# Sums of squares of the first norm on TensorE, and one rounding copy for both streams

## The chip, the cores and the metric

The kernel runs on one core of one Trainium2 chip. A core has a matrix engine (TensorE, PE in the profile, with its weight loads shown apart as PEld), VectorE (DVE), ScalarE (ACT), GpSimd (POOL), and SyncE (SP), whose queue issues the DMAs here. Each engine works through its own list in order and waits on semaphores of the others. The metric is device time of one execution in microseconds (us); lower is better.

## The reference

Two layers of a transformer-like trunk over 256 latent tokens and 256 context tokens of 1024 features, in fp32. Each layer is feed-forward, mixer, feed-forward. Every sublayer begins with a norm and a modulation:

```python
def rms_norm(x, g):
    y = x32 * lax.rsqrt(jnp.mean(x32 * x32, axis=-1, keepdims=True) + RMS_EPS)
    return (y * g.astype(jnp.float32)).astype(x.dtype)

def ffn_sublayer(h, m, g, w13, w2, base):
    hn = modulate(rms_norm(h, g), m[:, :, base], m[:, :, base + 1])   # h * (1 + scale) + shift
    return h + 0.5 * m[:, :, base + 2] * swiglu(hn, w13, w2)
```

The shifts, scales and gates m come from the conditioning vectors: `silu(cond) @ w + b`, one set for the latent tokens, one for the context tokens. The change is about the very first norm only, that of the first feed-forward of layer 0, which treats both streams together.

## The kernel before

Features lie on the 128 partitions, tokens along the row: `xl_all` holds the latent tokens as 8 d-tiles of 128x256, `xc_all` the context tokens. A matmul operand is split into a rounded part (`xh`, `whi`) and the rest (`xl`, `wlo`), and `mm3` makes three matmuls of them (L242 to L244).

The first feed-forward (`ffn_first`) begins while the inputs are still landing. Its list on ACT, DVE, PE and SP is written by hand in the order of the code (`tc.manual_schedule`); POOL's is not. It does this:

- `spread_c` puts the silu of the conditioning vectors on every partition as rows (PE transposes of L166, copies to `cvec`).
- `mod_cols(l, s, i, q, raw)` makes shift i and scale i of stream q (0 latent, 1 context). It consists of two calls of `mod_half`, each a DVE reduction over a 128x1024 weight tile (L197, out `jk`) and a short read of its accumulator; the second is followed by a small operation that makes the gain column `g` or `gc` (L204). Tile `mr` is the weight tile, from SP's DMAs.
- `squares(q, ...)` sums x*x over the features. ACT squares two halves of four d-tiles (L369, into `sq`). Then eng, POOL for the latent stream and DVE for the context stream, adds the d-tiles up (L373 to L376) until one 128x256 tile is left. `Rstd` sums its partitions with a matmul against a column `ones`, one per block of 128 tokens (L254), takes the root on ACT (L264), the reciprocal on DVE (L265), spreads it to all partitions with two transposes (L272) and copies it to `rs2` (`rs` in the profile, L279).
- `unit(k, q)` multiplies d-tile k of stream q by that (DVE, L386, into `xn`). `modulated(k)` applies gain and shift on ACT, first twice into the rounded `xh` (L392), then twice in place into the fp32 `xn` (L395). `low_part(k)` makes `xl` on DVE (L398). `split_hi` and `split_lo` split a quarter of the weight chunk of k (L406, L411).
- The loop over the 8 k-tiles (operand k for 8 column blocks at once): six blocks are fp32 matmuls of `xn` with the raw weights (L477, two instructions per matmul), two are `mm3` (outputs `p_3a`, `p_3b`). Ahead of the matmuls of k, each round writes unit, split and modulation of k + 1 and the modulation columns of k + 2.

`squares` is a generator: each `next` issues its next piece, so that other work can be put between. PSUM tiles come from two pools, three of two banks (`pair`) and two of one (`single`). After the loop come the rest of the first feed-forward (`pa`, `py`), the even mixer, two feed-forwards, the odd mixer, a last feed-forward and the final norm, which the change leaves as they are; their weight blocks are rounded on ACT by L98 and on DVE by L99.

Of the kernel before, what the change touches and what calls it, by code (L numbers as in the profile page):

```python
# [17 lines left out]
P = 128  # L18
# [33 lines left out]
def out_order(n, late):  # L52
    """Blocks (d, k) of an output projection: for the first n d-tiles the k-tile that is there last comes last."""
    early = [(d, k) for d in range(n) for k in range(KD) if k != late] + [(d, late) for d in range(n)]
    return early + [(d, k) for d in range(n, KD) for k in range(KD)]
# [6 lines left out]
class Stream:  # L62
    """Weight blocks in order of use: loaded two chunks at a time, then split into two float32r parts."""

# [41 lines left out]
    def block(self):  # L106
        """The next block of a run of blocks that starts with a chunk."""
        if self.at_chunk():
            self.run = self.get()
        j = self.blk % CH  # L110
        self.blk += 1
        return self.run[0][:, j, :], self.run[1][:, j, :]
# [3 lines left out]
def hybrid_trunk_kernel(ctx: ExitStack, tc: tile.TileContext, xc, cols_d, modw, wst, poolw_d,  # L116
# [15 lines left out]
    def single(name):  # L132
        return ps1.tile([P, 512], F32, tag="single", name=name)

    W = Stream(nc, wp_raw, wp_s, wst, 6, 3)

# [1 line left out]
    cols = cp.tile([P, NCOL], F32, name="cols")  # L138
# [16 lines left out]

    # silu of the conditioning vectors, as a row on every partition
    cvec = cp.tile([P, 2, D], F32, name="cvec")
# [16 lines left out]

# [1 line left out]
    mcol = {}  # L176
# [14 lines left out]
    def mod_half(l, s, i, q, h, raw):  # L191
        """Pairs 0..7 are (shift_i, scale_i); pairs 8..11 are gates (2(i-8), 2(i-8)+1)."""
        j = (i, 8 + i)[h] if i < 8 else 16 + 2 * (i - 8) + h
        m = mcol[l, s, q]
        junk = mp.tile([P, D], BF16, tag="junk", name=f"jk{l}{s}{i}{q}{h}", bufs=1)
        b = C_MODB + 72 * l + 24 * s + j
        nc.vector.tensor_tensor_reduce(  # L197
            out=junk, in0=raw[:, h, :], in1=cvec[:, q, :], scale=1.0,
            scalar=cols[:, b : b + 1], op0=ALU.mult, op1=ALU.add,
            accum_out=m[:, j : j + 1],  # L200
        )
        if h == 1 and i < 8:
            g0 = C_G + 24 * l + 8 * s + i
            nc.vector.scalar_tensor_tensor(  # L204
                gcol[l, s, q][:, i : i + 1], m[:, 8 + i : 9 + i], 1.0,
                cols[:, g0 : g0 + 1], ALU.add, ALU.mult,
            )
        elif i >= 8 and s != 1:
            nc.vector.tensor_scalar_mul(m[:, j : j + 1], m[:, j : j + 1], 0.5)
# [17 lines left out]
    def mod_credit(columns):  # L227
        """Issue modulation work for about so many columns per partition."""
        have[0] += columns
        while todo and have[0] >= 2 * len(todo[0][3]):  # L230
            have[0] -= 2 * len(todo[0][3])
            mod_next()

    def need_mods(l, s, lo, hi):
        """All columns of these pairs are issued by now."""
        while any(t[:2] == (l, s) and lo <= t[2] < hi for t in todo):
            mod_next()

# [1 line left out]
    def mm3(out, w, x, first, last):  # L240
# [5 lines left out]
    class Rstd:  # L246
        """Sums of squares over the d-tiles -> reciprocal root mean square of each token, on all partitions."""

# [10 lines left out]
        def root(self):  # L259
            """Tokens are on partitions here."""  # L260
            with tc.high_priority(offset=URGENT):
# [6 lines left out]
        def rows(self):  # L268
            """On all partitions, in PSUM."""
            n = self.n  # L270
# [12 lines left out]
    class Act:  # L283
        """Operand parts of one sublayer: columns 0..255 and a shift column twice, for one or two streams."""

# [12 lines left out]
        def feed(self, d, q=0):  # L298
            """Once x[d] is there."""
            with tc.high_priority(offset=URGENT):  # L300
# [41 lines left out]

# [1 line left out]
    def ffn_first():  # L344
        with tc.tile_pool(name="g0", bufs=1) as gp:
# [17 lines left out]

            def squares(q, xs_all, eng):
                """Yields after each piece of work, so that the caller can place it."""
                ts = []
                for h in range(2):
                    t = wp_s.tile([P, 4, T], F32, tag=("whi", "wlo")[h], name=f"sq4{q}{h}")
                    nc.scalar.activation(t, xs_all[:, 4 * h : 4 * h + 4, :], AF.Square)  # L369
                    ts.append(t)  # L370
                yield
                for t in ts:
                    eng.tensor_tensor(t[:, 0:2], t[:, 0:2], t[:, 2:4], ALU.add)  # L373
                eng.tensor_tensor(ts[0][:, 0:2], ts[0][:, 0:2], ts[1][:, 0:2], ALU.add)
                acc = ts[0][:, 2, :]
                eng.tensor_tensor(acc, ts[0][:, 0], ts[0][:, 1], ALU.add)  # L376
                yield
                Rstd([acc], 256, f"00{q}", None, q).root().spread()
                yield

            def unit(k, q):
                """x times its reciprocal root mean square"""
                if q == 0:
# [4 lines left out]
            def modulated(k):  # L388
                for q in range(2):
                    g, sh = gcol[0, 0, q][:, k : k + 1], mcol[0, 0, q][:, k : k + 1]  # L390
                    h = xh[:, k, q * 256 : q * 256 + 256]
                    nc.scalar.activation(h, xn[k][:, q, :], AF.Identity, bias=sh, scale=g)  # L392
                for q in range(2):
                    g, sh = gcol[0, 0, q][:, k : k + 1], mcol[0, 0, q][:, k : k + 1]
                    nc.scalar.activation(xn[k][:, q, :], xn[k][:, q, :], AF.Identity, bias=sh, scale=g)  # L395

            def low_part(k):
# [26 lines left out]
            with tc.manual_schedule(engines=MANUAL):  # L424
# [9 lines left out]
                spread_c()  # L434
                lat, con = squares(0, xl_all, nc.gpsimd), squares(1, xc_all, nc.vector)
                next(lat)
                mod_cols(0, 0, 0, 0, raws[0])
                next(lat)
                next(con)
                mod_cols(0, 0, 0, 1, raws[0])  # L440
                next(con)
                next(lat)
                mod_half(0, 0, 1, 0, 0, raws[1])
                unit(0, 0)
                next(con)
                mod_half(0, 0, 1, 0, 1, raws[1])
                unit(0, 1)
                prs = [pair(f"p0_{j}") for j in range(3)]
                pts = [t[:, j, :] for t in prs for j in range(2)] + [single("p0_3a"), single("p0_3b")]
                split_hi(0)  # L450
                modulated(0)
                split_lo(0)
                mod_half(0, 0, 1, 1, 0, raws[1])
                low_part(0)
                mod_half(0, 0, 1, 1, 1, raws[1])
                for k in range(KD):
# [5 lines left out]
                    if not last:  # L462
                        for q in range(2):
                            unit(k + 1, q)
                        split_hi(k + 1)
                        modulated(k + 1)
                        if k + 2 < KD:
# [63 lines left out]

# [1 line left out]
    def even_mixer(act):  # L533
        with tc.tile_pool(name="mix", bufs=2) as ap_:
# [51 lines left out]

            # windowed means less the token, then the per-group map
            def pool_means():
# [38 lines left out]
            def put(name, i, t, n):  # L627
                """t [P, n streams, 258] with its shift column -> float32r parts, tokens along the row."""
                h = ap_.tile([P, n * T], F32R, tag=f"{name}h", name=f"{name}h{i}")
# [44 lines left out]
            def scores(i, b):  # L674
                """Scores of two heads, and the steps of their softmax."""
                (qh, ql), (kh_, kl_) = qs[i], ks_[i]
# [68 lines left out]

            # first pair of heads: the norm's factor is still under way
            wq, wk = W.get(), W.get()
# [87 lines left out]
    class OutProj:  # L835
        """Output projection of a mixer; the operand's last k-tile may come late."""

# [34 lines left out]

# [1 line left out]
    def ffn(act, l, s, gp, nxt_of, rate1, rate2):  # L874
# [43 lines left out]

# [1 line left out]
    def odd_mixer(act, gp, rate):  # L920
# [70 lines left out]
def _blocks(w, cols):  # L991
    """w (1024, n) -> [len(cols), 128, 8 * 128]: chunk per group of 128 output features, k-tiles along the row."""
    import numpy as np
# [121 lines left out]
```

## Time and profile before

| | |
|---|---|
| median of three executions | 1209.8 us (1209.5, 1209.8, 1213.49) |
| the profiled execution, its span | 1211.3 us |
| mean granted TensorE clock | 0.986 |
| first norm: POOL's four adds (L373 to L376) | 9.73 to 16.26 us |
| first matmul of the loop over k (L477) | 23.20 us |
| DVE's reductions L197, whole program | 184, 236.4 us |

The page of the profile gives busy times by engine, the chain of work that ended last and groups of like instructions. A row of the timeline reads: start in us from the span's beginning, duration in us, engine, line, operation, output<-inputs, shape, count of merged instructions, and in brackets the idle time before it with what ended it. A row of waits reads: who waited <- for whom: us in total, times, longest. The profile merges neighbours of one line, so the step between them is worked out from a row's length and count. "Granted clock" is the share of full speed that TensorE's clock gate passed; where the trace has no record yet (before 7.6 us) the column shows 1.00.

### The profile page before, as it was taken

How to read it: one execution, taken by the hardware profiler on the slowest of the kernel's cores; microseconds unless marked ns; L12 is line 12 of the kernel's file. 1: busy time of each engine (PE TensorE's matmuls, PEld its weight loads, DVE VectorE, ACT ScalarE, POOL GpSimd, SP SyncE). 2: the span in 40 equal slices, each digit the busy share in tenths (PEclk: the TensorE clock that was granted, in tenths of full speed). 3: DMA queues.
4: the chain of work that ended last, by engine and by line, in shares of the span. 5: the costliest groups of instructions: out<-in, count | busy, mean ns of one | idle time of the engine just before them, and what ended most of it. 6: DMA issues, size and time to landing. Idle time of an engine off the chain costs nothing.

```text
span 1211.3 us, 19831 instructions
## 1 busy us (share of the span) xinstructions
PE 1180.3 (97%) x8134; PEld 1084.0 (89%) x8134; DVE 918.6 (76%) x1463; ACT 535.7 (44%) x804; POOL 21.2 (2%) x23
## 2 busy tenths in 40 slices
PE   4999999999999999999999999999999999999997
PEld 2568888888888988999999999999999999999997
DVE  8967686676788697877887897887887887676653
ACT  4352321223234444655544545454545456545542
POOL 2000000000000040000000000000000000000000
PEclk7999999999999999999999999999999999999999
DMA  7755454356666653235667886766786555554551
GB/s 275 247 212 173 173 176 174 139 215 272 244 259 229 223 133 88 70 125 213 226 236 256 307 334 219 256 228 243 281 322 232 174 182 191 185 174 180 195 182 35
DMA packets 45801, 250.72 MB, mean 207 GB/s; under 512 B 12944, under 2 KB 13328, under 8 KB 17552
## 3 DMA queue, kind: packets, MB, share of 16 engines
q1 hardware_dynamic: 45712, 249.48, 57.6%
q8 instruction: 63, 1.03, 0.3%
q14 instruction: 26, 0.21, 0.0%
HBM read 248.41 MB, written 1.05 MB: 206 GB/s over the span
## 4 chain that ended last, share of the span: by engine, by line
PE 94%; DVE 2%; DMA 1%; issue 1%; ACT 0%; SPq 0%; DVEq 0%; ACTq 0%
PE pf L243 11%; PE pf L242 10%; PE pf L244 10%; PE pa L243 6%; PE pa L242 6%; PE pa L244 6%; PE pz L244 5%; PE pz L243 5%; PE pz L242 5%; PE p L477 4%; PE py L243 3%; PE py L244 3%; PE py L242 3%; PE pwo L242 1%; PE pwo L243 1%; PE pc L243 1%
## 5 line engine op out<-in xcount | busy, mean ns | idle before, releaser
L98 ACT CAST whi<-raw 128x1024 fp32r<-128x1024 f32 x312 | 327.1, 1049 | 460.6 <-PE pa L243 121.0
L99 DVE TENSOR_TENSOR wlo<-raw,whi 128x1024 fp32r<-128x1024 f32 x312 | 380.2, 1223 | 177.1 <-ACT whi L98 176.5
L242 PE MATMUL pf<-ah,whi 128*128 128x258 f32 x1056 | 298.4, 283 | 0.0
L243 PE MATMUL pf<-al,whi 128*128 128x258 f32 x1056 | 298.4, 283 | 0.0
L244 PE MATMUL pf<-ah,wlo 128*128 128x258 f32 x1056 | 297.6, 282 | 0.0
L197 DVE CUSTOM_DVE_ANT_0 jk<-mr,cvec,cols 128x1024 bf16<-128x1024 f32 x184 | 236.4, 1285 | 1.7
L244 PEld LDWEIGHTS pf<-ah,wlo 128*128 128x128 f32 x1056 | 200.2, 190 | 0.0
L243 PEld LDWEIGHTS pf<-al,whi 128*128 128x128 f32 x1056 | 200.1, 190 | 0.0
L242 PEld LDWEIGHTS pf<-ah,whi 128*128 128x128 f32 x1056 | 199.7, 189 | 0.0
L243 PE MATMUL pz<-gl,whi 128*128 128x256 f32 x528 | 148.3, 281 | 0.0
L244 PE MATMUL pz<-gh,wlo 128*128 128x256 f32 x528 | 148.3, 281 | 0.0
L242 PE MATMUL pz<-gh,whi 128*128 128x256 f32 x528 | 148.3, 281 | 0.0
L243 PE MATMUL pa<-xl,whi 128*128 128x512 f32 x288 | 114.0, 396 | 0.0
L242 PE MATMUL pa<-xh,whi 128*128 128x512 f32 x288 | 113.7, 395 | 0.0
L244 PE MATMUL pa<-xh,wlo 128*128 128x512 f32 x288 | 113.6, 394 | 0.0
L242 PEld LDWEIGHTS pz<-gh,whi 128*128 128x128 f32 x528 | 99.5, 188 | 0.0
L244 PEld LDWEIGHTS pz<-gh,wlo 128*128 128x128 f32 x528 | 99.5, 188 | 0.0
L243 PEld LDWEIGHTS pz<-gl,whi 128*128 128x128 f32 x528 | 99.5, 188 | 0.0
L243 PE MATMUL py<-gl,whi 128*128 128x512 f32 x176 | 69.6, 396 | 0.0
L244 PE MATMUL py<-gh,wlo 128*128 128x512 f32 x176 | 69.6, 396 | 0.0
L242 PE MATMUL py<-gh,whi 128*128 128x512 f32 x176 | 69.6, 395 | 0.0
L242 PEld LDWEIGHTS pa<-xh,whi 128*128 128x128 f32 x288 | 54.1, 188 | 13.1
(233 smaller groups left out, 1796.5 us busy)
## 6 DMA issues: line engine op xcount, KB each, us to landing
raw<-in_wst SPq DMA_DIRECT2D x156, 1024.0 KB, 4.9
mr<-in_modw SPq DMA_DIRECT2D x64, 1024.0 KB, 4.9
mr<-in_modw SPq DMA_DIRECT2D x16, 512.0 KB, 4.8
raw<-in_wst SPq DMA_DIRECT2D x8, 512.0 KB, 6.7
bias<-in_rpb SPq DMA_DIRECT2D x32, 64.0 KB, 5.9
xl_all<-in_xc SPq DMA_DIRECT2D x2, 512.0 KB, 7.0
xc_all<-in_xc SPq DMA_DIRECT2D x2, 512.0 KB, 8.7
out<-done SPq DMA_DIRECT2D x3, 256.0 KB, 2.8
```

Of the source, the lines that this page charges most:

```text
L98: nc.scalar.copy(hi, src)
L99: self.last = nc.vector.tensor_tensor(lo, src, hi.bitcast(F32), ALU.subtract).ins
L197: nc.vector.tensor_tensor_reduce(out=junk, in0=raw[:, h, :], in1=cvec[:, q, :], scale=1.0, scalar=cols[:, b : b + 1], op0=ALU.mult, op1=AL ...
L242: nc.tensor.matmul(out, wh, xh, start=first, stop=False)
L243: nc.tensor.matmul(out, wh, xl, start=False, stop=False)
L244: nc.tensor.matmul(out, wl, xh, start=False, stop=last)
L477: nc.tensor.matmul(pts[j], wf[:, j * P : j * P + P], f32, start=first, stop=last)
```

## The change

In the first norm the squares are no longer added up by POOL and DVE. Each squared d-tile goes to PE at once: for each half (four d-tiles) and each of two token blocks an fp32 matmul of the squares as weights against `ones` adds into one PSUM column (L373 of the changed file), 16 matmuls per stream. The root, the reciprocal and the spread stay (now L379, L380, L383, L386), with a PSUM pair in place of a single. The order of the code around it changes: both streams' columns of tile 0 come ahead of the squares; the latent spread stands behind the context stream's sums; all columns of tile 1 come behind the two units of tile 0. `modulated` writes the fp32 `xn` of both streams first (L399) and then makes `xh` of both with one copy (L400); `split_hi` comes behind it.

```diff
-            def squares(q, xs_all, eng):
-                ts = []
+            def squares(q, xs_all):
+                pt = pair(f"pn00{q}")
                 for h in range(2):
                     t = wp_s.tile([P, 4, T], F32, tag=("whi", "wlo")[h], name=f"sq4{q}{h}")
                     nc.scalar.activation(t, xs_all[:, 4 * h : 4 * h + 4, :], AF.Square)
-                    ts.append(t)
+                    for j in range(4):
+                        for b in range(2):
+                            nc.tensor.matmul(
+                                pt[:, b, 0:1], t[:, j, b * P : b * P + P], ones,
+                                start=h == j == 0, stop=h == 1 and j == 3,
+                            )
+                    yield
+                r = tp.tile([P, 5], F32, tag="root", name=f"rt00{q}")
+                nc.scalar.activation(r[:, 0:2], pt[:, :, 0], AF.Sqrt, bias=eps_t[:, 0:1], scale=1.0 / D)
+                nc.vector.reciprocal(r[:, 0:2], r[:, 0:2])
                 yield
-                for t in ts:
-                    eng.tensor_tensor(t[:, 0:2], t[:, 0:2], t[:, 2:4], ALU.add)
-                eng.tensor_tensor(ts[0][:, 0:2], ts[0][:, 0:2], ts[1][:, 0:2], ALU.add)
-                acc = ts[0][:, 2, :]
-                eng.tensor_tensor(acc, ts[0][:, 0], ts[0][:, 1], ALU.add)
+                for b in range(2):
+                    nc.tensor.transpose(
+                        pt[:, 0, b * P : b * P + P], r[:, b : b + 1].to_broadcast([P, P]), ident
+                    )
+                nc.scalar.copy(rs2[:, q, 0:256], pt[:, 0, 0:256])
                 yield
-                Rstd([acc], 256, f"00{q}", None, q).root().spread()
-                yield
...
             def modulated(k):
                 for q in range(2):
                     g, sh = gcol[0, 0, q][:, k : k + 1], mcol[0, 0, q][:, k : k + 1]
-                    h = xh[:, k, q * 256 : q * 256 + 256]
-                    nc.scalar.activation(h, xn[k][:, q, :], AF.Identity, bias=sh, scale=g)
-                for q in range(2):
-                    g, sh = gcol[0, 0, q][:, k : k + 1], mcol[0, 0, q][:, k : k + 1]
                     nc.scalar.activation(xn[k][:, q, :], xn[k][:, q, :], AF.Identity, bias=sh, scale=g)
+                nc.scalar.copy(xh[:, k, 0:512], xn[k].rearrange("p a b -> p (a b)"))
...
-                lat, con = squares(0, xl_all, nc.gpsimd), squares(1, xc_all, nc.vector)
+                for q in range(2):
+                    mod_cols(0, 0, 0, q, raws[0])
+                lat, con = squares(0, xl_all), squares(1, xc_all)
                 next(lat)
-                mod_cols(0, 0, 0, 0, raws[0])
                 next(lat)
                 next(con)
-                mod_cols(0, 0, 0, 1, raws[0])
                 next(con)
                 next(lat)
-                mod_half(0, 0, 1, 0, 0, raws[1])
+                next(lat)
                 unit(0, 0)
                 next(con)
-                mod_half(0, 0, 1, 0, 1, raws[1])
+                next(con)
                 unit(0, 1)
...
+                modulated(0)
                 split_hi(0)
-                modulated(0)
+                mod_cols(0, 0, 1, 0, raws[1])
                 split_lo(0)
-                mod_half(0, 0, 1, 1, 0, raws[1])
                 low_part(0)
-                mod_half(0, 0, 1, 1, 1, raws[1])
+                mod_cols(0, 0, 1, 1, raws[1])
...
+                        modulated(k + 1)
                         split_hi(k + 1)
-                        modulated(k + 1)
```

What this does to the lists of the engines, at the three places that matter later. In the names, `pn` is the PSUM tile of the norm, `rt` root and reciprocal, `jk` a reduction, `m` and `g` its columns (`mc`, `gc` for the context stream), and the number behind a name tells tiles of one name apart.

PE, between the transposes of `spread_c` and the first matmuls of the loop. Before:

```order
L254 MATMUL pn_208<-ones,sq_182 128x1 x2
L272 MATMUL pn_208<-ident,rt_211 128x128 x2
L254 MATMUL pn_221<-ones,sq_195 128x1 x2
L272 MATMUL pn_221<-ident,rt_224 128x128 x2
L477 MATMUL p_0_234<-xn_219,raw_150 128x512 x2
```

and in the changed kernel:

```order
L373 MATMUL pn_192<-ones,sq_193 128x1 x8
L373 MATMUL pn_192<-ones,sq_203 128x1 x8
L373 MATMUL pn_213<-ones,sq_214 128x1 x8
L373 MATMUL pn_213<-ones,sq_224 128x1 x8
L383 MATMUL pn_192<-ident,rt_234 128x128 x2
L383 MATMUL pn_213<-ident,rt_242 128x128 x2
L482 MATMUL p_0_249<-xn_240,raw_150 128x512 x2
```

Four matmuls became 32, and the latent stream's transposes moved behind the context stream's matmuls.

DVE, from the end of the context stream's adds to the first reductions for tile 1. Before:

```order
L376 TENSOR_TENSOR sq_195<-sq_195 128x256
L265 RECIPROCAL rt_211<-rt_211 128x2
L197 ISA jk_217,m_97<-mr_152,cvec,cols 128x1024
L197 ISA m_97 128x1
L386 TENSOR_TENSOR xn_219<-xl_all,rs_92 128x256
L265 RECIPROCAL rt_224<-rt_224 128x2
L197 ISA jk_230,m_97<-mr_152,cvec,cols 128x1024
L197 ISA m_97 128x1
L204 SCALAR_TENSOR_TENSOR g_98<-m_97,cols 128x1
L386 TENSOR_TENSOR xn_219<-xc_all,rs_92 128x256
L411 TENSOR_TENSOR wlo_240<-raw_150,whi_239 128x256
```

and in the changed kernel:

```order
L204 SCALAR_TENSOR_TENSOR gc_110<-mc_109,cols 128x1
L380 RECIPROCAL rt_234<-rt_234 128x2
L394 TENSOR_TENSOR xn_240<-xl_all,rs_92 128x256
L380 RECIPROCAL rt_242<-rt_242 128x2
L394 TENSOR_TENSOR xn_240<-xc_all,rs_92 128x256
L197 ISA jk_260,m_97<-mr_152,cvec,cols 128x1024
L197 ISA m_97 128x1
L197 ISA jk_262,m_97<-mr_152,cvec,cols 128x1024
L197 ISA m_97 128x1
L204 SCALAR_TENSOR_TENSOR g_98<-m_97,cols 128x1
L416 TENSOR_TENSOR wlo_258<-raw_150,whi_257 128x256
```

The adds are gone, and the two reductions that stood ahead of the second unit of tile 0 moved behind it.

ACT, from the second copy to `rs2` to the end of tile 0. Before:

```order
L279 COPY rs_92<-pn_221 128x256
L406 CAST whi_239<-raw_150 128x256
L392 ACTIVATE xh_139<-xn_219,m_97,g_98 128x256
L392 ACTIVATE xh_139<-xn_219,mc_109,gc_110 128x256
L395 ACTIVATE xn_219<-xn_219,m_97,g_98 128x256
L395 ACTIVATE xn_219<-xn_219,mc_109,gc_110 128x256
```

and in the changed kernel:

```order
L386 COPY rs_92<-pn_213 128x256
L399 ACTIVATE xn_240<-xn_240,m_97,g_98 128x256
L399 ACTIVATE xn_240<-xn_240,mc_109,gc_110 128x256
L400 CAST xh_139<-xn_240 128x512
L411 CAST whi_257<-raw_150 128x256
```

The fp32 operand moved to the front, and the split of the weights behind the rounding. SP's list of DMAs is the same. Behind the eighth tile only the neighbours of the first PSUM reads change places: before, two of the next phase's rounding copies (L98) stood ahead of the modulation of the last tile on ACT, and now all of them stand behind it.

## Prediction

> **What bounds the kernel now.** I read the page's totals and chain of waits first, then who TensorE (PE) waits for, then the timeline of the first 80 us, which is all that the change touches. The page:
>
> ```profile
> span 1211.3 us, 19831 instructions
> PE 1180.3 (97%) x8134; PEld 1084.0 (89%) x8134; DVE 918.6 (76%) x1463; ACT 535.7 (44%) x804; POOL 21.2 (2%) x23
> PE 94%; DVE 2%; DMA 1%; issue 1%; ACT 0%; SPq 0%; DVEq 0%; ACTq 0%
> ...
> L98 ACT CAST whi<-raw 128x1024 fp32r<-128x1024 f32 x312 | 327.1, 1049 | 460.6 <-PE pa L243 121.0
> ```
>
> PE carries the end (L98, ACT's rounding of a weight chunk, is used below). Its waits in the first 80 us, and the largest after 78 us:
>
> ```profile
> PE pn L254 <- POOL sq L376: 9.2, 1, 9.2
> PE p L477 <- ACT xn L395: 2.7, 1, 2.7
> ...
> PE pT L720 <- DVE sm L709: 2.8, 3, 1.8
> ```
>
> From 23 us on PE hardly waits, so the rest of the program moves as one block with the end of the first eight k-tiles (L477, then L242 to L244). The question is only how far that end moves. The timeline of the first norm, then of one k-tile, then of the last one:
>
> ```profile
> 8.60 1.06 ACT L369 ACTIVATE sq<-xl_all 128x1024 f32<-128x1024 f32 x1 [0.82 <-DMA xl_all<-in_xc]
> ...
> 10.10 2.17 DVE L197 CUSTOM_DVE_ANT_0 jk<-mr,cvec,cols 128x1024 bf16<-128x1024 f32 x1
> 12.71 1.06 ACT L369 ACTIVATE sq<-xc_all 128x1024 f32<-128x1024 f32 x1 [0.22 <-DMA xc_all<-in_xc]
> ...
> 17.37 0.26 ACT L264 ACTIVATE rt<-pn,eps 128x2 f32<-128x2 f32 x1 [3.60 <-PE pn L254]
> 17.66 0.17 DVE L265 RECIPROCAL rt<-rt 128x2 f32<-128x2 f32 x1 [0.39 <-ACT rt L264]
> 17.88 0.69 PE L272 MATMUL pn<-ident,rt 128*128 128x128 f32 x2 [0.55 <-DVE rt L265]
> 18.61 0.37 ACT L279 COPY rs<-pn 128x256 f32<-128x256 f32 x1 [0.98 <-PE pn L272]
> 21.08 0.42 DVE L386 TENSOR_TENSOR xn<-xc_all,rs 128x256 f32<-128x256 f32 x1
> 23.20 7.84 PE L477 MATMUL p<-xn,raw 128*128 128x512 f32 x12 [2.74 <-ACT xn L395]
> 25.18 0.42 DVE L386 TENSOR_TENSOR xn<-xl_all,rs 128x256 f32<-128x256 f32 x1
> ...
> 32.25 0.42 DVE L386 TENSOR_TENSOR xn<-xl_all,rs 128x256 f32<-128x256 f32 x1
> 32.59 0.42 DVE L386 TENSOR_TENSOR xn<-xc_all,rs 128x256 f32<-128x256 f32 x1
> 32.92 1.28 DVE L197 CUSTOM_DVE_ANT_0 jk<-mr,cvec,cols 128x1024 bf16<-128x1024 f32 x1
> 33.21 0.58 ACT L392 ACTIVATE xh<-xn,mc,gc 128x256 fp32r<-128x256 f32 x1
> 34.20 0.59 ACT L395 ACTIVATE xn<-xn,mc,gc 128x256 f32<-128x256 f32 x1
> 39.33 0.42 DVE L386 TENSOR_TENSOR xn<-xl_all,rs 128x256 f32<-128x256 f32 x1
> ...
> 64.96 5.31 PE L477 MATMUL p<-xn,raw 128*128 128x512 f32 x12
> 67.63 0.42 DVE L386 TENSOR_TENSOR xn<-xl_all,rs 128x256 f32<-128x256 f32 x1
> 69.57 0.58 ACT L395 ACTIVATE xn<-xn,mc,gc 128x256 f32<-128x256 f32 x1
> 71.49 5.31 PE L477 MATMUL p<-xn,raw 128*128 128x512 f32 x12
> ...
> 72.52 1.28 ACT L416 ACT_TABLE_LOAD   x1
> 73.82 0.60 ACT L416 ACTIVATE s<-p 128x512 f32<-128x512 f32 x1
> 74.44 0.69 DVE L417 TENSOR_TENSOR s<-s,p 128x512 f32<-128x512 f32 x1 [0.68 <-ACT s L416]
> ```
>
> Two periods are to be seen. PE takes 71.49 - 64.96 = 6.53 us for a k-tile; VectorE (DVE) takes 39.33 - 32.25 = 7.08, with no idle time. DVE is the slower one, and PE does not notice because it starts late and half of its first tile runs at half clock. The lead melts tile by tile: for the last one the operand is ready at 69.57 + 0.58 = 70.15 and PE takes it at 71.49, so 1.34 us are left. After the change this loop is judged by DVE's clock, not by PE's.
>
> **The change, part by part.** I follow one time: U, the start of the second unit() on DVE (21.08 before).
>
> *Behind U.* The two mod_half calls that stood between the two units (1.28 us and a 0.08 read each, one small L204) now stand behind them, so from U to the first unit of the next tile DVE has a full tile's list without its first unit: from 32.59 to 39.33, 6.74 us, against 25.18 - 21.08 = 4.10 before. Cost: 2.64 us on DVE, on the path, since all seven later tiles follow in DVE's rhythm: 67.63 - 25.18 = 42.45 us from tile 1's unit to tile 7's.
>
> *ACT's order.* xh took two ACTs ahead of xn's two; now xn's two come first and one 128x512 copy makes xh. The operand of the six fp32 column blocks is ready 34.20 - 33.21 = 0.99 us earlier per tile. xh comes at about the old end of xn; xl on DVE waits for it but stands behind two 1.28 us reductions, so that costs nothing, and PE needs xl only 5 us into the tile. The split of the weight slice moves behind the copy: same cover. Two rounding copies of the next phase and its table load now stand behind the last tile's work on ACT. From that tile's unit on DVE: 1.5 until xn, two small copies (under 0.6 each), two of 1.05 (L98), 1.28 for the table, 0.60 for the first L416, 0.69 for L417 makes 7.4 us until the first PSUM pair is free; PE wants it after 1.6 + 6.53 = 8.1. I put that at 0, with 1 as its other end.
>
> *The break-even.* PE may start the last tile at U + 6.74 + 42.45 + (70.15 - 67.63) - 0.99 + 0.04 = U + 50.76. That is the old 71.49 if U = 20.73. PE itself, from its first tile at about U + 1.1, would be there at U + 1.1 + 7 x 6.53 = U + 46.8, and half clock during 5 us of its first tile, as before, adds 2.5; so DVE decides. Shift of the whole program = U - 20.73.
>
> *Ahead of U: removed.* POOL's four adds and DVE's four (L373 to L376). While POOL ran, DVE's own operations grew (2.17 us at 10.10, where the same operation takes 1.28 at 32.92). Without them DVE is through with its four first reductions at about 10.10 + 1.28 + 0.2 = 11.6 us and then has nothing until the first reciprocal; that is no gain by itself, as the norm now waits for PE.
>
> *Ahead of U: added.* 2 streams x 2 halves x 4 d-tiles x 2 token blocks = 32 fp32 matmuls with one moving column. Each is two instructions with a weight load of its own: 64, against 8 before. Their rows, at half and at full clock:
>
> ```profile
> 18.15 0.98 PEld L254 LDWEIGHTS pn<-ones,sq 128*128 128x128 f32 x4
> ...
> 410.87 0.98 PEld L254 LDWEIGHTS pn<-ones,acc 128*128 128x128 f32 x8
> 1204.16 0.43 PE L272 MATMUL pnf<-ident,rtf 128*128 128x128 f32 x2 [0.55 <-DVE rtf L265]
> ```
>
> One load lasts about 0.33 at half clock and 0.19 at full clock, and they overlap: the step is (0.98 - 0.33) / 3 = 0.215 us, and (0.98 - 0.19) / 7 = 0.113 us. All four sums stand ahead of the first transpose in PE's queue, so the latent stream waits for the context stream's 32 instructions as well. Chain from PE's last step T to U at full clock: transposes 0.43, copy 0.37, unit 0.34, reciprocal 0.17, transposes 0.43, copy 0.37, and 0.04 for each hand-over: about 2.3 us (2.8 with 0.69 us transposes). The squares on ACT end 9.66 to 13.77, so PE starts at about 9.7 and then sets T itself.
>
> The Trainium skill (TensorE: Matmul & The Clock Gate, LDWEIGHTS) gives a weight load P / 1.2 ns, 107 ns for 128 columns, whatever the gate does; with 107 ns the 64 would take an estimated 6.8 us, U would be 18.8 and the shift -1.9. The L254 rows disagree at half clock (0.215), and the measurement is taken.
>
> **Which clock PE has there.** Stretches on the gate's grid; columns: length, busy time of PE, PEld, DVE, ACT, POOL with counts, granted clock, DMA share, GB/s:
>
> ```profile
> 4.21:7.62 3.41, 2.95 (x13) 2.08 (x12) 2.92 (x5) 1.48 (x4) 0.00 (x0) 1.00 1.00 353
> 7.62:11.04 3.42, 0.00 (x0) 0.00 (x0) 3.35 (x6) 2.06 (x3) 1.31 (x1) 1.00 1.02 379
> 11.04:14.45 3.41, 0.00 (x0) 0.00 (x0) 3.38 (x5) 2.32 (x3) 3.19 (x3) 0.50 1.02 354
> ...
> 17.86:21.28 3.42, 2.02 (x8) 1.54 (x8) 3.27 (x8) 1.42 (x5) 0.00 (x0) 0.50 0.89 362
> 21.28:24.69 3.41, 1.50 (x2) 0.84 (x3) 3.27 (x6) 2.16 (x5) 0.00 (x0) 0.50 0.01 5
> 24.69:28.10 3.41, 3.41 (x5) 1.35 (x4) 3.34 (x8) 2.37 (x5) 0.00 (x0) 0.50 0.52 144
> 28.10:31.52 3.42, 3.42 (x10) 1.70 (x9) 3.35 (x8) 0.00 (x0) 0.00 (x0) 1.00 0.80 319
> ```
>
> A stretch with PE busy 2.95 or 3.41 us is followed by full clock, one with 2.02 or less by half. What no row shows is whether a dense stream of one-column matmuls counts as busy: the array streams next to nothing, only weights load. So T is bounded from both sides. Full clock throughout: 64 x 0.113 = 7.2, T = 16.9, U = 19.2, shift -1.5. It doesn't count: 12 instructions at full clock until 11.04, then 52 x 0.215 = 11.2, T = 22.2, U = 25.0, shift +4.3. It counts: 12 at full clock, the stretch 11.04 to 14.45 at half clock for 16, the remaining 36 x 0.113 = 4.1, T = 18.5, U = 20.8, shift +0.1. I take this one, because the page's busy time of PE and PEld alike would be full there, and that is what the other stretches follow. If the grid lies otherwise against the start, the half-clock part lasts about 2.4 to 6.4 us instead of 3.4 (it ends with the first stretch that lies mostly behind 9.7), which moves U by -0.5 to +1.5.
>
> **Sum.** 2.64 (two halves behind U) - 0.99 (xn first) - 1.34 (lead used up) + (20.8 - 21.08) (U) + 0.04 = +0.1 us on the profiled 1211.3, which lies between the three times 1209.5, 1209.8 and 1213.49. Against their median, with a little for the grid: 1210.0 us.
>
> **Rivals.**
> 1. One-column matmuls leave the gate at half clock: +4.3, 1214.1 us, slower by 0.35%. For it: a gate that guards the array has little to see there; the stretch 17.86 to 21.28, with four of them among four transposes, kept half clock. Against: that stretch was only 59% busy. It passes 0.3% (U = 24.3) once about 45 of the 64 run at half clock. Beside it: the Trainium skill (TensorE: Matmul & The Clock Gate, Part 4) says that transposes do not count as busy in the same way; the trace disagrees, since PE has only the transposes of L166 from 4.21 to 7.62, and full clock followed.
> 2. The gate stays open from the first square on: -1.5, 1208.3 us. Against: PE did nothing from 7.62 to 11.04, and now would start at 9.7, so 1.3 us of that stretch are busy; 2.02 of one did not open the gate.
> 3. DVE's loop is no longer the bound, and PE runs eight full-clock tiles from U + 1.1 = 20.3: the end of the eighth moves from 71.49 + 6.53 = 78.0 to 72.5, 1204.3 us. That needs DVE's period below 6.53 us with the same instructions; nothing speaks for it.
> 4. The work is only moved: what leaves POOL and DVE ahead of U comes back as PE instructions ahead of U and DVE work behind it. That is the forecast itself, no change.
>
> **Chances.** A measurement of this kernel can tell about 0.3% (3.6 us) from no change. Forecast, with all positions of the grid: 0.51. Rival 1: 0.35, a quarter of it inside 0.3%. Rival 2: 0.06. Rival 3: 0.04. Something late that I put at 0 (the PSUM pair, a landing): 0.04, slower. That makes faster 0.04, same 0.51 + 0.06 + 0.09 = 0.66, slower 0.26 + 0.04 = 0.30. The forecast's own range is 1208.5 to 1212; with rival 1 the range goes to 1214.8, and down to 1208.0 for rival 2.
>
> **What would show it.** In the new profile: 64 instructions of L373 on PE from about 9.7 us, and their spacing after 14.5 us, 0.11 or 0.21, decides between forecast and rival 1. U near 20.8 or 25.0. PE waits for ACT xn in each of tiles 1 to 7, about 0.5 us each, where it had one wait of 2.7. The reductions before 12 us all last 1.28. PE is at the L242 rows of pa at about 78.1 (before 78.0). The prediction is wrong if that time differs by more than 2 us with a spacing of 0.11, or if the block after it does not move along.

## Result: 0.38% slower, by the first rival

| | before | changed |
|---|---|---|
| median of 14 executions | 1209.94 us | 1214.95 us |
| ratio, 95% interval | | 1.0038 [1.0026, 1.0051] |
| the profiled execution, its span | 1211.3 us | 1212.8 us |
| U, second unit of tile 0 on DVE | 21.08 us | 24.88 us |
| first matmul of pa, the end of the loop | 78.01 us | 82.33 us |

The ratio is 4.6 us [3.1, 6.2]. The loop ends 4.3 us later: this is what the first rival said (+4.3, U = 25.0), not the forecast (+0.1, U = 20.8). The median lies 0.15 us above the upper end of the range; the ratio times the median before, 1214.5, lies inside it.

The page after, totals and the chain by engine:

```profile
span 1212.8 us, 19918 instructions
PE 1189.3 (98%) x8190; PEld 1092.3 (90%) x8190; DVE 912.8 (75%) x1459; ACT 532.5 (44%) x796; POOL 15.0 (1%) x19
PE 91%; DVE 6%; DMA 1%; issue 1%; ACT 0%; SPq 0%; DVEq 0%; ACTq 0%
```

POOL and DVE are 6 us lighter each, as meant. PE is busy 9 us longer, and the kernel is slower. DVE's share of the chain rose from 2% to 6%: the loop over the k-tiles now ends on DVE's list. The timeline after, in the places quoted before (columns as there):

```profile
9.31 12.91 PE L373 MATMUL pn<-ones,sq 128*128 128x1 f32 x64 [2.23 <-ACT sq L370]
...
15.73 0.17 DVE L380 RECIPROCAL rt<-rt 128x2 f32<-128x2 f32 x1 [4.21 <-ACT rt L379]
22.09 0.67 PE L383 MATMUL pn<-ident,rt 128*128 128x128 f32 x2
24.88 0.42 DVE L394 TENSOR_TENSOR xn<-xc_all,rs 128x256 f32<-128x256 f32 x1 [1.19 <-ACT rs L386]
25.99 7.79 PE L482 MATMUL p<-xn,raw 128*128 128x512 f32 x12 [1.55 <-ACT xn L399]
31.62 0.42 DVE L394 TENSOR_TENSOR xn<-xl_all,rs 128x256 f32<-128x256 f32 x1
...
74.08 0.42 DVE L394 TENSOR_TENSOR xn<-xl_all,rs 128x256 f32<-128x256 f32 x1
75.68 5.42 PE L482 MATMUL p<-xn,raw 128*128 128x512 f32 x12 [0.27 <-ACT xn L399]
82.33 0.39 PE L242 MATMUL pa<-xh,whi 128*128 128x512 f32 x1
```

The 64 sum instructions last 12.9 us. The latent reciprocal is done at 15.9, and its transposes come at 22.09, behind the context stream's sums: 6 us in which DVE and ACT have nothing. From U on the times are those of the prediction's sum: the next unit 31.62 - 24.88 = 6.74 behind it, the last 42.46 behind that, pa 82.33 - 24.88 = 57.45 behind U. The clock meanwhile, on the gate's grid:

```profile
6.92:10.33 3.41, 1.18 (x10) 1.02 (x10) 3.30 (x8) 2.49 (x3) 0.00 (x0) 1.00 1.01 406
10.33:13.74 3.41, 3.41 (x18) 3.41 (x18) 1.16 (x3) 2.32 (x3) 0.00 (x0) 0.50 1.02 393
13.74:17.16 3.42, 3.42 (x17) 3.42 (x18) 0.17 (x1) 0.26 (x1) 0.00 (x0) 0.50 1.03 420
17.16:20.57 3.41, 3.41 (x17) 3.41 (x18) 0.00 (x0) 0.00 (x0) 0.00 (x0) 0.50 0.93 376
20.57:23.98 3.41, 2.42 (x11) 2.01 (x12) 0.50 (x2) 0.54 (x2) 0.00 (x0) 0.50 0.00 0
...
27.40:30.81 3.41, 3.41 (x5) 1.35 (x4) 3.34 (x8) 0.00 (x0) 0.00 (x0) 0.50 0.02 5
30.81:34.22 3.41, 3.41 (x10) 1.65 (x9) 3.34 (x8) 2.02 (x4) 0.00 (x0) 1.00 0.40 102
```

Three whole stretches have PE and its weight loads busy from end to end, and each is followed by half clock. The first stretch full of L482 is followed by full clock. The page's busy time of PE is therefore not what the gate goes by.

The delay passes on as one block: `pq`, the mixer's first output, starts 4.31 us later too. Its row in the timeline of the kernel before:

```profile
402.32 0.28 PE L242 MATMUL pq<-ah,whi 128*128 128x258 f32 x1
```

and of the changed one:

```profile
406.63 0.28 PE L242 MATMUL pq<-ah,whi 128*128 128x258 f32 x1
```

The spans of the two profiled executions differ by only 1.5 us because the one before has three stretches of half clock later in the mixer (from 444.5, 478.7 and 526.5 us) and the one after has one, from 450.65. That differs from execution to execution, so I compare places ahead of these stretches, and times by their ratios.

### The profile page after: what moved, and what is told of

It reads as the page before. It is cut to its first block, busy times and chain, and to the rows that moved or that the text cites. A ratio compares the mean times of both kernels' runs of the same rounds, so it can differ in the third digit from the quotient of the medians.

```text
span 1212.8 us, 19918 instructions
## 1 busy us (share of the span) xinstructions
PE 1189.3 (98%) x8190; PEld 1092.3 (90%) x8190; DVE 912.8 (75%) x1459; ACT 532.5 (44%) x796; POOL 15.0 (1%) x19
## 4 chain that ended last, share of the span: by engine, by line
PE 91%; DVE 6%; DMA 1%; issue 1%; ACT 0%; SPq 0%; DVEq 0%; ACTq 0%
PE pf L243 11%; PE pf L242 10%; PE pf L244 10%; PE pa L243 6%; PE pa L242 6%; PE pa L244 6%; PE pz L243 5%; PE pz L242 5%; PE pz L244 5%; PE py L242 3%; PE py L244 3%; PE py L243 3%; DVE jk L197 3%; PE pwo L242 1%; PE pc L243 1%; PE pc L242 1%
## 5 line engine op out<-in xcount | busy, mean ns | idle before, releaser
L98 ACT CAST whi<-raw 128x1024 fp32r<-128x1024 f32 x312 | 327.2, 1049 | 454.7 <-PE pa L243 122.8
L244 PE MATMUL pf<-ah,wlo 128*128 128x258 f32 x1056 | 298.1, 282 | 0.0
L244 PEld LDWEIGHTS pf<-ah,wlo 128*128 128x128 f32 x1056 | 200.4, 190 | 0.0
L244 PE MATMUL pz<-gh,wlo 128*128 128x256 f32 x528 | 148.6, 281 | 0.0
L244 PE MATMUL pa<-xh,wlo 128*128 128x512 f32 x288 | 113.7, 395 | 0.0
L244 PEld LDWEIGHTS pz<-gh,wlo 128*128 128x128 f32 x528 | 99.7, 189 | 0.0
L244 PE MATMUL py<-gh,wlo 128*128 128x512 f32 x176 | 69.7, 396 | 0.0
```

The lines of the kernel that those rows point to most:

```text
L98: nc.scalar.copy(hi, src)
L244: nc.tensor.matmul(out, wl, xh, start=False, stop=last)
```

## Experiments

The markers are U and the first matmul of pa; the difference between them tells what binds the loop, and U tells what the norm costs.

**e1: is it the clock, and what opens it?** The same 64 instructions and weight loads, with 128 columns streaming instead of one:

```diff
-                                pt[:, b, 0:1], t[:, j, b * P : b * P + P], ones,
+                                pt[:, b, 0:128], t[:, j, b * P : b * P + P], ones_w[:, 0:128],
```

> The changed kernel with 128 equal columns of ones instead of one in each of its 32 sum matmuls, so that the array streams as long as a weight load lasts; nothing else is changed. Markers: U (second unit of tile 0 on DVE; 21.08 before, 24.88 after) and the first matmul of pa (78.01 before, 82.33 after). Theory A, the gate counts columns that stream and not weight loads: full clock from about 13.7 us, the rest of the 64 instructions at 0.113 instead of 0.213, U near 20.5, pa near 77.9, about 1210.5 us, no change against the kernel before. Rival B, the half clock has another cause (the idle gap ahead, the start of the program): 0.213 throughout, U 24.9, pa 82.3, about 1214.6. Rival C, 128 columns cost time of their own beside the weight load: a step well over 0.213, pa later than 84.

Measured: U = 20.83, time 1.0001 [0.9992, 1.0011] of the kernel before. The sums, U and the start of pa in its timeline (L244 is the first of pa's three lines here, as the lines have moved by two):

```profile
9.82 8.92 PE L375 MATMUL pn<-ones_w,sq 128*128 128x128 f32 x64 [3.11 <-ACT sq L372]
...
20.83 0.42 DVE L396 TENSOR_TENSOR xn<-xc_all,rs 128x256 f32<-128x256 f32 x1 [0.93 <-ACT rs L388]
78.29 0.39 PE L244 MATMUL pa<-xh,whi 128*128 128x512 f32 x1
```

The first two stretches of its sums on the gate's grid, columns as before:

```profile
9.59:13.01 3.42, 3.19 (x15) 3.19 (x16) 2.21 (x5) 2.45 (x4) 0.00 (x0) 0.50 1.01 386
13.01:16.42 3.41, 3.41 (x32) 3.41 (x32) 0.17 (x1) 1.16 (x2) 0.00 (x0) 1.00 1.03 420
```

Sixteen instructions in the stretch at half clock, 32 in the next: 127 more columns cost nothing, open the gate and halve the step. Rivals B and C fall, and the whole loss goes with the half clock. With U at 20.83 the time equals the one before, as the break-even of 20.73 said. The other runs repeat it: with one column all 64 instructions of e3 and e7 stay at half clock, with 128 columns the step halves after the first full stretch in e5 and e8 too. What comes along with the columns (more products, more writes to PSUM) is not told apart from the streaming itself.

**e2: 64 columns.**

> The same with 64 columns: at half clock the array streams half of each 0.213 us step. Theory A with a threshold between the 59% that left half clock and the 83% that opened the gate in the kernel before: half clock stays, U 24.9, pa 82.3. If a weight load counts in part, or the threshold lies under 50%: as with 128 columns, U near 20.5 and pa near 77.9.

Measured: U = 25.97, pa at 83.42, one execution 1213.94 us. The half clock stays through all 64 instructions. This trace has no clock record before 31.56 us, so it is read from their step of 0.21 us:

```profile
9.50 13.92 PE L375 MATMUL pn<-ones_w,sq 128*128 128x64 f32 x64 [2.46 <-ACT sq L372]
...
25.97 0.43 DVE L396 TENSOR_TENSOR xn<-xc_all,rs 128x256 f32<-128x256 f32 x1 [1.19 <-ACT rs L388]
83.42 0.39 PE L244 MATMUL pa<-xh,whi 128*128 128x512 f32 x1
```

U is 1.1 later than in the changed kernel since here the gate had not opened behind the transposes of L166 either: in the changed kernel it had, and its first ten sums, ahead of 10.33 us, took 0.11 each. Weight loads that run without a gap plus columns that stream half the time do not open it; the point lies between 64 and 128 columns per load.

**e3: tile 1's reductions ahead of the norm.** One column as in the changed kernel:

```diff
-                for q in range(2):
-                    mod_cols(0, 0, 0, q, raws[0])
+                for i in range(2):
+                    for q in range(2):
+                        mod_cols(0, 0, i, q, raws[i])
...
-                mod_cols(0, 0, 1, 0, raws[1])
...
-                mod_cols(0, 0, 1, 1, raws[1])
```

> The changed kernel (one column) with all four reductions of tile 1 moved ahead of the norm on DVE, where it idles. Theory: with them behind U, DVE's rhythm sets the loop's end (U + 57.45); ahead of U PE sets it: first L482 at 26.0 as in the changed kernel, half clock in the first tile worth 2.5, pa at 26.0 + 8 x 6.53 + 2.5 = 80.7 instead of 82.3. Rival, the order on DVE costs nothing: 82.3. The sums stay at half clock in both.

Measured: pa at 81.82, one execution 1213.15 us.

```profile
25.63 0.43 DVE L394 TENSOR_TENSOR xn<-xc_all,rs 128x256 f32<-128x256 f32 x1 [1.19 <-ACT rs L386]
...
26.74 8.06 PE L481 MATMUL p<-xn,raw 128*128 128x512 f32 x12 [1.55 <-ACT xn L399]
...
81.82 0.39 PE L242 MATMUL pa<-xh,whi 128*128 128x512 f32 x1
```

U is 0.75 later than in the changed kernel (half clock from the first sum on), but pa comes 56.19 behind it instead of 57.45. It lies at 26.74 + 8 x 6.53 + 2.8: PE binds here, and the first tile's half clock counts again. So both reductions behind U cost 1.3 us by this run. The changed kernel's own rows give 1.6: PE alone, from 25.99 with a first tile of 7.79 instead of 5.31, would be at pa at 25.99 + 8 x 6.53 + 2.48 = 80.7, and it is there at 82.33. The rest of their 2.6 was hidden by PE's own half clock.

**e4: ACT's new order alone**, with the old norm (the diff's `modulated` and `split_hi` lines).

> The kernel before with only the new order on ACT (fp32 operand first, one copy for both streams, split behind it); the norm is the old one. Theory: the first L477 comes about 1.0 earlier (22.15 instead of 23.20) and pa with it, 77.0, or down to DVE's bound at 75.8 if the clock opens a stretch earlier. Rival, ACT's order is worth nothing because PE was not waiting for it later on: pa 78.0.

Measured: pa at 77.20, one execution 1206.84 us. The first matmul came as expected, and pa 0.2 later than the 77.0 expected of PE. On DVE a wait is new:

```profile
20.94 0.42 DVE L386 TENSOR_TENSOR xn<-xc_all,rs 128x256 f32<-128x256 f32 x1
22.98 0.42 DVE L408 TENSOR_TENSOR wlo<-raw,whi 128x256 fp32r<-128x256 f32 x1 [1.62 <-ACT whi L403]
...
26.53 0.42 DVE L386 TENSOR_TENSOR xn<-xl_all,rs 128x256 f32<-128x256 f32 x1
```

and in PE's rows the first and the last place:

```profile
22.05 8.01 PE L474 MATMUL p<-xn,raw 128*128 128x512 f32 x12 [1.73 <-ACT xn L391]
...
77.20 0.39 PE L242 MATMUL pa<-xh,whi 128*128 128x512 f32 x1
```

In the old list DVE splits the weight slice right behind the unit, and now waits 1.62 us for the copy that went behind on ACT. The next unit is 1.35 later than before, so DVE's bound for pa is now 26.53 + 42.45 + 1.57 + 6.53 = 77.1, and PE's, with its first tile of 8.01, is 22.05 + 8 x 6.53 + 2.70 = 77.0. The two nearly meet: the new wait has used up DVE's lead, but cost pa at most 0.2.

**e7: the new norm alone**, with ACT's old order in the changed kernel (the reverse of e4's edit).

> The changed kernel with ACT's old order (xh twice, then xn twice, split ahead). Theory: DVE's rhythm binds, so the 0.99 us by which xn is later falls through to the end: pa at U + 58.4 instead of U + 57.45, 83.3 with U at 24.9. Rival, ACT's order is covered: U + 57.4.

Measured: one execution 1215.94 us.

```profile
26.72 0.43 DVE L394 TENSOR_TENSOR xn<-xc_all,rs 128x256 f32<-128x256 f32 x1 [1.19 <-ACT rs L386]
...
85.15 0.39 PE L242 MATMUL pa<-xh,whi 128*128 128x512 f32 x1
```

pa comes 58.43 behind U. ACT's order is worth 0.98 us where DVE binds, as the prediction had it (U itself is late here: the sums start at 10.25 instead of 9.31, and the gate had closed at 9.91, ahead of all of them).

**e5: both causes taken away.** 128 columns and e3's edit together.

> 128 columns of ones (full clock for the sums) and tile 1's reductions ahead of the norm, both at once. If the two causes are the whole of it, U stays near 20.8, DVE's rhythm no longer binds, PE runs eight tiles from 21.9 at 6.53: pa at 74.2 if the gate stays open from the sums on (as it did in e1), up to 76.7 if it closes for the first tile; against 78.0 before: 2 to 4 us faster, 1204 to 1206. Rival, something else binds the loop: pa at 78 as in e1, 1208.

Measured: 1.0018 [1.0009, 1.0027] of the kernel before, a miss:

```profile
16.17 1.28 DVE L199 CUSTOM_DVE_ANT_0 jk<-mr,cvec,cols 128x1024 bf16<-128x1024 f32 x1 [3.88 <-DMA mr<-in_modw]
...
21.68 0.16 DVE L382 RECIPROCAL rt<-rt 128x2 f32<-128x2 f32 x1
24.20 0.42 DVE L396 TENSOR_TENSOR xn<-xc_all,rs 128x256 f32<-128x256 f32 x1 [0.93 <-ACT rs L388]
```

Tile 1's weights land at about 16 us. DVE waits 3.88 for them, with the latent reciprocal behind them in its list, so the spread comes late (PE waits 2.02 for the reciprocal) and U is 24.20. About 1.1 of the 3.4 us against e1 is not this: the sums end at 19.88 here and at 18.74 there. In e3 the sums at half clock had covered the landing. The part that was meant holds: pa comes 55.1 behind U.

**e6: the ones as weights**, so that no transposes are needed:

```diff
+                        nc.tensor.matmul(
+                            pt[:, 0:256], ones_w, t[:, j, :], start=h == j == 0, stop=h == 1 and j == 3
+                        )
...
+                nc.vector.reciprocal(r, r)
```

Here r is `rs2[:, q, 0:256]`, on all partitions; e3's edit is in it too.

> The ones as weights (128x128) and the squares as 256 moving columns: the sum arrives on every partition at once, without transposes; root on ACT and reciprocal on DVE work on 128x256; tile 1's reductions ahead of the norm. 32 instructions of 0.213 us at full clock instead of 64 of 0.113, all of them streaming. If the gate counts streaming columns, the sums end near 18, U is 19.2 (reciprocal of 256 columns 0.4 us) to 20.5 (1.7 us), pa 72.5 to 75.5, 1203 to 1205.5. Rival: the wide reciprocal or a closed gate takes it back, pa 76 to 78.

Measured: 1.0027 [1.0017, 1.0037], pa at 80.20, a miss. The sums were over by about 18.2, as expected. The reciprocal of 128x256 takes ten times that of 128x2 and stands behind the reductions again, and twice on the path. PE meanwhile idles 7.36 us, so the first tile runs at half clock for the most part, 7.59 instead of 5.31 (the rival's other half):

```profile
20.57 1.75 DVE L381 RECIPROCAL rs<-rs 128x256 f32<-128x256 f32 x1
22.35 0.43 DVE L389 TENSOR_TENSOR xn<-xl_all,rs 128x256 f32<-128x256 f32 x1
22.70 1.75 DVE L381 RECIPROCAL rs<-rs 128x256 f32<-128x256 f32 x1
...
25.59 7.59 PE L476 MATMUL p<-xn,raw 128*128 128x512 f32 x12 [7.36 <-ACT xn L394]
```

**e8: 128 columns, and reductions where their weights are there.** The two latent reductions stand between the latent reciprocal and the latent unit:

```diff
                 next(lat)
+                mod_cols(0, 0, 1, 0, raws[1])
                 next(lat)
                 unit(0, 0)
...
-                mod_cols(0, 0, 1, 0, raws[1])
+                mod_cols(0, 0, 1, 1, raws[1])
                 split_lo(0)
                 low_part(0)
-                mod_cols(0, 0, 1, 1, raws[1])
```

> 128 columns of ones as in e1, and the two latent reductions of tile 1 between the latent reciprocal and the latent unit, where DVE idles and their weights have landed (about 16 us in e5); the two context reductions directly behind U. U should stay near 20.8 as in e1. DVE's bound for pa falls by the 2.8 us of two reductions, from U + 57.45 to U + 54.7 = 75.5; PE's own is 21.9 + 8 x 6.53 = 74.2, with up to 2.5 more if the gate closes for the first tile. So pa 75.5 to 76.7 against 78.0 before: 1.5 to 2.5 us faster, 1206 against 1208.3. Rival, the reductions' weights land late again and hold up the unit as in e5: U 23 or later, pa near 78.

Measured: 0.9988 [0.9978, 0.9997] of the kernel before.

```profile
15.31 0.17 DVE L382 RECIPROCAL rt<-rt 128x2 f32<-128x2 f32 x1 [3.91 <-ACT rt L381]
...
20.64 0.43 DVE L396 TENSOR_TENSOR xn<-xc_all,rs 128x256 f32<-128x256 f32 x1 [0.93 <-ACT rs L388]
...
75.36 0.39 PE L244 MATMUL pa<-xh,whi 128*128 128x512 f32 x1
```

pa comes 54.72 behind U, as worked out, 2.65 us ahead of the kernel before. By the ratio the program gains 1.5 us.

**e9: the old norm with ACT's new order, DVE's split moved behind the reductions.** Against e4:

```diff
-                split_lo(0)
                 mod_half(0, 0, 1, 1, 0, raws[1])
-                low_part(0)
                 mod_half(0, 0, 1, 1, 1, raws[1])
+                split_lo(0)
+                low_part(0)
```

> The kernel before with ACT's new order, as e4, and DVE's split of the first weight slice behind the two context reductions of tile 1 instead of ahead of them, where it waited for ACT in e4. The old norm on POOL and DVE stays. PE's bound: first L477 at 22.05, pa at 22.05 + 8 x 6.53 + 2.5 = 76.8 against 78.0 before; DVE's bound 75.7. So about 1.2 us faster, 1207.1 against 1208.3. Rival: nothing gained over e4, 77.2.

Measured: 0.9987 [0.9979, 0.9996].

```profile
22.16 7.21 PE L474 MATMUL p<-xn,raw 128*128 128x512 f32 x12 [1.73 <-ACT xn L391]
...
76.40 0.39 PE L242 MATMUL pa<-xh,whi 128*128 128x512 f32 x1
```

The wait of e4 is gone, and pa is 1.6 us ahead of the kernel before: 1.0 by the first matmul, 0.6 because the gate opened earlier in the first tile (7.21 against 7.84). The 0.8 us against e4 is this luck of the grid (7.21 against 8.01), not the wait. e8 and e9 cannot be told apart by time; each is about 0.1% faster than the kernel before.

## Why the prediction was right or wrong

- *What bounds, and the break-even:* right. DVE's rhythm of 7.08 decides in the last three tiles; pa = U + 57.45 in the changed kernel, in e1 and in e2, whatever U is, and at U = 20.8 the time is that of before.
- *Which clock PE has there:* wrong, and this is the step that failed. I put "it counts" first, because the page's busy time agreed with the gate in every other stretch. In all those stretches, loads and streams come together, so they could not tell the two apart; the one place where they part was the one to be predicted. The term U = 20.8 was 24.88. e1 shows that streaming columns are what was missing, with the number of loads the same: there U is 20.83. The stated range reached to 1214.8 only because it took in the first rival; the time near its end owes nothing to the forecast's mechanism.
- *The other end of that bound:* 52 x 0.215 and 2.8 us of tail gave U = 25.0, against 24.88. The first rival had mechanism, place and size. I gave it 0.35 against 0.51 for the forecast, though no row showed that loads alone count.
- *Two reductions behind U, 2.64:* the shift on DVE is right (6.74 against 4.10). Its price was 1.3 (e3) to 1.6 (the changed kernel's own rows), as PE's half clock in the first tile would have bound next.
- *ACT's order, -0.99:* right where DVE binds, 0.98 (e7). Not foreseen is that the old list on DVE would have waited for the moved split (e4); the change escapes that only because the reductions stand in front of it.
- *PSUM pair and table load, 0:* right. L422 ends with the first pair 7 us behind the last unit, PE wants it after 8.2.
- *Waits of PE in tiles 1 to 7:* half right. With the half clock in the first tile PE was late itself, and waits only in tiles 5 to 7, 0.2 to 0.3 us each. In e1, where that tile runs at full clock, it waits in each of tiles 1 to 7, 0.26 to 0.43 us.
- *The price of a weight load:* right. The step was 0.213 at half clock, where I had put 0.215 (the row's 0.65 / 3 is 0.217), and 0.112 at full clock, where I had put 0.113; all 64 took 12.9 us. The Trainium skill (TensorE: Matmul & The Clock Gate, LDWEIGHTS) would give an estimated 6.8; its 107 ns is near the step at full clock and half of that at half clock. Part 4 of that page of the Trainium skill, by which transposes do not count as busy in the same way, was the right kind of doubt; in these runs it is not the transposes but the one-column matmuls.

## To carry to other kernels

Here sums by a one-column matmul were priced by the weight load, and at half clock since a long row of them stood alone: PE busy from end to end did not open the gate. Widening the moving operand up to what a load hides, 128 columns, cost nothing and opened it (e1). Before moving work to an engine that is idle, ask what becomes the bound: here DVE's order behind the norm, and the landing of the weights in front of it (e5), decided as much as the work itself.

## What was not expected of the hardware

- Three stretches of 3.41 us with PE and PEld 100% busy at one column, and more than 13 us at 64 columns per load (e2), left half clock; the first stretch with 128 columns, 93% busy, opened it. Where between 64 and 128 columns it turns, and whether loads count in part, stays open.
- An open gate stayed open in e1 over a stretch with PE busy 2.54 of 3.41 us, and so was open in the next (the two stretches behind those shown under e1):

```profile
16.42:19.83 3.41, 2.54 (x23) 2.29 (x22) 0.43 (x2) 0.54 (x2) 0.00 (x0) 1.00 1.02 414
19.83:23.25 3.42, 1.74 (x5) 0.87 (x6) 2.46 (x5) 2.39 (x5) 0.00 (x0) 1.00 0.19 74
```

- What closes it is not the busy time alone either. In e1 it stayed open after the second of these stretches too, with 1.74 of 3.42 us busy; in the kernel before, far behind the loop, a stretch with 2.01 us busy closed it:

```profile
523.04:526.45 3.41, 2.01 (x14) 1.55 (x13) 1.60 (x4) 0.97 (x3) 0.00 (x0) 1.00 0.19 79
526.45:529.86 3.41, 3.41 (x17) 3.41 (x17) 3.12 (x9) 3.25 (x8) 0.00 (x0) 0.50 0.02 5
```

- Whether the transposes of L166 open the gate for the first sums is luck of the grid: it opened behind 2.89 us or more of them in a stretch (2.89 in e6, 2.95 before) and not behind 2.79 or less (2.79 in e2, 2.23 in e3, whose grid is worked out backwards from the first clock record in steps of 3.413 us). For one-column sums this is about 1 us of U, so U in single executions tells no finer differences than that; pa behind U does.
- DVE's reciprocal took 0.16 us for 128x2 and 1.75 us for 128x256, where a multiply of the same size takes 0.43 (e6).
